# Splitting the last chunk's down projection by tokens: 384 with features on the partitions, 128 with tokens on the partitions

## The chip, the cores and the metric

The kernel runs on one core of one Trainium2 chip. The metric is the device time of one execution in microseconds (us); the kernel before has a median of 2044.64 us over 3 runs (2043.89 to 2045.69). Lower is better. TensorE does the matrix products and transposes into PSUM, VectorE (DVE) and ScalarE (ACT) the elementwise work, GpSimd (POOL) some products and the accumulating DMAs, and SyncE (SP) issues most DMAs, in the order in which they were written down.

## The reference

One layer of an encoder on 512 tokens with 2048 features in float32: a mixer (convolution and neighbourhood attention), then a gated MLP, then a final RMSNorm. The change touches only the last lines:

```python
up = depthwise_conv(jnp.einsum("bsd,df->bsf", xn, w_up[l]), ffn_dw_w[l], ffn_dw_b[l])
gate, val = jnp.split(up, 2, axis=-1)
x = x + jnp.einsum("bsf,fd->bsd", jax.nn.silu(gate) * val, w_down[l])    # 5632 -> 2048
return rms_norm(x, final_norm_g)     # x * rsqrt(mean(x*x over features) + eps) * g
```

## The kernel before

Activations lie transposed: features on the 128 partitions, the 512 tokens along the free dimension. 2048 features are 16 tiles `x2[0..15]` of 128 x 512 each. The hidden dimension 5632 is 44 tiles of 128, taken in 11 chunks of 4 (`NCH`, `CH`).

Matrix products keep float32 accuracy with three fast matmuls: weight and activation are each split into a rounded high part and a low rest, and `mm3` (L123) adds high x high, high x low and low x high into one PSUM bank (lines L126, L127, L128). So one product of a 128 x 128 weight tile with 4 hidden tiles (`hs[0..3]`, each a pair high and low) is 12 matmuls.

For chunks 0 to 9 the down projection (`down`, L830) makes one PSUM bank of 128 features x 512 tokens per feature tile d, copies it (L841) and has POOL add it by an accumulating DMA onto the residual in DRAM (`xd[d]`, L842). The last of these, for d = 8 to 15, run at the very end of the loop, between them the weights of the last chunk are loaded (`last_weights`, L865: 8 DMAs of 512 KB, split into `dh` and `dl` by ACT at L870 and DVE at L871). The residual comes back from DRAM as `x2[d]` (`reload`, L861).

The last chunk is not added through DRAM. `half` (L896) is called for tokens 0 to 255, then for tokens 256 to 511. For each d it makes 12 matmuls with a moving operand of 256 tokens into a bank of the pool `psm` (3 banks), DVE adds the bank onto `x2[d]` (L903), ACT squares it (L168), and DVE adds the square to `acc` (L169). `rsqrt_steps` (L171) then sums `acc` over the partitions by matmuls with ones (`st`, L183), takes 1/sqrt(mean + eps) with one Newton step on 128 x 2 values (L188 to L193), and spreads the result to all partitions by a matmul with a diagonal matrix (`dg` L200, `rb` L204). `finish` (L883) multiplies two feature tiles with the gain g3 and with `rb` (L892 on DVE, or for some pairs L889 on ACT and L890 on POOL) and stores 128 x 2 x 256 values to the output (L894, from SP's queue).

The statistics and the finishing of the first half are written between the feature tiles of the second half (`first_half`, L916). Those of the second half stand after its last matmul: nothing else is left then.

The order of instructions on each engine is made by a scheduler from priorities in writing order; each engine then runs its own list strictly in that order.

Of the kernel before, what the change touches and what calls it, by code (L numbers as in the profile page):

```python
# [28 lines left out]
EPS = 1e-6  # L29

KD = D // P
# [7 lines left out]
NB = GW // BLK  # L39
KC0 = [0, 8, 24, 32]  # L40
H = S // 2
CH = 4
NCH = NF // CH
NT = 79
# [19 lines left out]


@with_exitstack
def layer(ctx: ExitStack, tc: tile.TileContext, xT, xG, w_in, w_v, w_out, w_up, w_down, par, tab, out):
# [55 lines left out]
    def mm3(ps, w, wk, mh, ml, start, stop):  # L123
        hi, lo = w[:2]
        a = slice(wk * P, (wk + 1) * P)
        nc.tensor.matmul(ps, hi[:, a], mh, start=start, stop=False)  # L126
        nc.tensor.matmul(ps, hi[:, a], ml, start=False, stop=False)  # L127
        return nc.tensor.matmul(ps, lo[:, a], mh, start=False, stop=stop)  # L128
# [34 lines left out]
    def sum_sq(acc, src, first, to=slice(0, S)):  # L163
        if first:
            nc.scalar.activation(acc, src, AF.Square)
        else:
            q = t2("sq")[:, to]
            nc.scalar.activation(q, src, AF.Square)  # L168
            nc.vector.tensor_add(acc, acc, q)  # L169

    def rsqrt_steps(accs, n, name, to=slice(0, S), keep=True, by_token=None):  # L171

        if not isinstance(accs, tuple):
            accs = accs,
        m = (to.stop - to.start) // P
        banks = [psa.tile([P, S], F32, tag="po", name="st")]
        if len(accs) > 1:
            banks.append(psa.tile([P, 2, S], F32, tag="sc", name="st")[:, 0])
        v, r, y = (sm.tile([P, S // P], F32, tag="rs" + c, name="rs" + c)[:, :m] for c in "vry")
        for b, acc in enumerate(accs):  # L180
            ps = banks[b][:, :m]
            for i in range(m):
                nc.tensor.matmul(ps[:, i:i + 1], acc[:, to.start + i * P:to.start + (i + 1) * P], ones[:, 0:1],  # L183
                                 start=True, stop=True)
            if b:
                nc.vector.scalar_tensor_tensor(v, ps, 1.0 / n, v, op0=ALU.mult, op1=ALU.add)
            else:
                nc.vector.tensor_scalar(v, ps, 1.0 / n, EPS, op0=ALU.mult, op1=ALU.add)  # L188
        nc.scalar.activation(r, v, AF.Sqrt)
# [3 lines left out]
        nc.vector.scalar_tensor_tensor(y, y, 1.5, r, op0=ALU.add, op1=ALU.mult)  # L193

        if by_token is not None:
            by_token.append(y)
        if not keep:
            dg = t2("dg")
            for i in range(m):
                nc.vector.tensor_scalar(dg[:, i * P:(i + 1) * P], ident, y[:, i:i + 1], None, op0=ALU.mult)  # L200
            yield
            both = [psa.tile([P, S], F32, tag="tr", name="rb", bufs=2)[:, :m * P] for _ in range(2)]
            for ps in both:
                nc.tensor.matmul(ps, ones, dg[:, :m * P], start=True, stop=True)  # L204
            return both

        yh, yl = (sm.tile([P, S // P], dt, tag="rs" + c, name="rs" + c) for c, dt in (("h", F32R), ("l", F32)))
        nc.vector.tensor_copy(yh, y)
        nc.vector.tensor_sub(yl, y, yh.bitcast(F32))
        ds = []  # L210
        for part in (yh.bitcast(F32), yl):
            ds.append(t2("dg", F32R))
            nc.vector.tensor_mul(ds[-1].rearrange("p (i k) -> p i k", k=P), ident.unsqueeze(1).broadcast_to([P, m, P]),
                                 part.unsqueeze(2).broadcast_to([P, m, P]))
        yield
        ps = psa.tile([P, S], F32, tag="po", name="st")
# [6 lines left out]
    def rsqrt_value(g):  # L223
        while True:
            try:
                next(g)
            except StopIteration as e:
                return e.value

    xs, x1 = [], []
    acc1 = t2("acc1")
# [41 lines left out]
    for step in ORDER:  # L275
        if step == "v":
            half = next(v_)
# [3 lines left out]
        i = next(a_ if step == "a" else q_)  # L281
# [265 lines left out]
    p, n = -1, 0  # L547
# [20 lines left out]
    x2 = []  # L568
# [124 lines left out]
    def down_units(c, i, at):  # L693

        n = U // CH
        if not c:
# [161 lines left out]
    n = CH  # L858
    x2, ws = [], []

    def reload(d):  # L861
        x2.append(t2("x2"))
        nc.sync.dma_start(x2[d], xd[d])
# [15 lines left out]
        last_weights(len(ws))  # L879
    for d in range(KD // 2, KD):  # L880
        reload(d)

    def finish(ds, r, to, apart=False):  # L883

        o = t2("fin").rearrange("p (i t) -> p i t", i=2)[:, :len(ds)]
        for i, d in enumerate(ds):
            x, g = x2[d][:, to], pc("g3", d)
            if apart:
                nc.scalar.activation(x, x, AF.Copy, scale=g)  # L889
                nc.gpsimd.tensor_mul(o[:, i], x, r)  # L890
            else:
                nc.vector.scalar_tensor_tensor(o[:, i], x, g, r, op0=ALU.mult, op1=ALU.mult)  # L892
        i = ds[0] % 2
        nc.sync.dma_start(out[to.start // H, ds[0] // 2][:, i:i + len(ds)], o)  # L894

    def half(to, between):  # L896

        acc = t2("acc3")
        for d in range(KD):
            ps = psm.tile([P, S], F32, tag="mm", name="pd")[:, to]  # L900
            for k in range(n):
                mm3(ps, ws[d], k, hs[k][0][:, to], hs[k][1][:, to], k == 0, k == n - 1)
            nc.vector.tensor_add(x2[d][:, to], x2[d][:, to], ps)  # L903
            if d < KD - 1:
                sum_sq(acc[:, to], x2[d][:, to], d == 0, to=to)
            else:
                q = t2("sq")
                nc.scalar.activation(q[:, to], x2[d][:, to], AF.Square)
            between(d)
        return rsqrt_steps((acc, q), D, "rstd3", to=to, keep=False)  # L910

    h0, h1 = slice(0, H), slice(H, S)
    stats, todo = half(h0, lambda d: None), [(d, d + 1) for d in range(0, KD, 2)]
    r0 = []

    def first_half(d):  # L916

        if d == 0:
            next(stats)
        elif d == 2:  # L920
            try:
                next(stats)
            except StopIteration as e:
                r0.append(e.value[0])
        elif d > 2 and d % 5 != 4 and todo:
            finish(todo.pop(0), r0[0], h0)

    r, rp = rsqrt_value(half(h1, first_half))
    assert not todo

    rb = t2("rb")[:, h1]
    nc.scalar.activation(rb, rp, AF.Copy)
    for ds in [(0,), (1,)] + [(d, d + 1) for d in range(2, KD, 2)]:
        apart = ds[0] in (4, 10)
        finish(ds, rb if apart else r, h1, apart)


def _cols(a):
# [66 lines left out]
```

## Time and profile before

| | us |
|---|---|
| median of 3 runs | 2044.64 (2043.89 to 2045.69) |
| profiled execution, its time | 2047.1 |
| its span, first to last instruction | 2045.3 |
| PE busy in the span | 2025.5 |
| DVE busy | 1672.8 |
| ACT busy | 1035.4 |
| POOL busy | 156.2 |
| first matmul of `half` starts | 1981.96 |
| last DVE add of a PSUM bank onto x2 (L903) starts | 2030.14 |

The profile is of one execution. Its span is 1.8 us shorter than that execution's time, and that execution is 2.46 us above the median of the runs. Times inside the profile count from the span's start. A matmul's row shows when it starts and how long it lasts, and consecutive matmuls overlap: what a matmul costs a full TensorE is the distance from its start to the next one's.

### The profile page before, as it was taken

Reading aid. Unit: us, or ns where it says so; the run is one execution under the profiler, and the core shown is the slowest. Engines: PE = TensorE matmul, PEld = TensorE weight load, DVE = VectorE, ACT = ScalarE, POOL = GpSimd, SP = SyncE. Lnnn points to the kernel's source line nnn. Section 1 sums busy time; section 2 is a strip of 40 time slices with the busy share of each in tenths; the row PEclk is TensorE's granted clock in tenths of the full one; section 3 lists DMA queues with packets and bytes.
Section 4 is the critical chain, followed back from the end, with each engine's and each line's share of the span. In section 5 each row is a group of like instructions: output and inputs, shape, how many; then the busy total and the mean of one; then the engine's idle time right before and its main releaser. Section 6 shows DMA issues by size and latency. Waiting matters only on the chain.

```text
span 2045.3 us, 28399 instructions
## 1 busy us (share of the span) xinstructions
PE 2025.5 (99%) x10752; PEld 1731.9 (85%) x10752; DVE 1672.8 (82%) x2319; ACT 1035.4 (51%) x1662; POOL 156.2 (8%) x186
## 2 busy tenths in 40 slices
PE   9999999999999999999999999999999999999997
PEld 7888888878888898888888888888888888888887
DVE  7986888878577898888888788788888888889876
ACT  6323234347346555555555555555554555555552
POOL 0000000000001001111111111111111111110110
PEclk9999999999999999999999999999999999999998
DMA  7232333336347435566566565665555566555682
GB/s 254 82 104 91 114 95 103 108 119 216 104 121 178 113 114 144 118 151 145 124 144 144 135 133 145 138 134 142 131 146 143 124 146 146 130 134 127 149 212 83
DMA packets 97209, 275.38 MB, mean 135 GB/s; under 512 B 10928, under 2 KB 11696, under 8 KB 97072
## 3 DMA queue, kind: packets, MB, share of 16 engines
q1 hardware_dynamic: 71712, 227.40, 36.6%
q0 software_dynamic: 25216, 46.15, 15.6%
q8 instruction: 85, 1.39, 0.3%
q14 instruction: 52, 0.43, 0.1%
q10 hardware_dynamic: 144, 0.01, 0.0%
HBM read 218.99 MB, written 54.53 MB: 134 GB/s over the span
## 4 chain that ended last, share of the span: by engine, by line
PE 95%; DVE 2%; ACT 1%; DMA 1%; issue 1%; SPq 0%; DVEq 0%; ACTq 0%
PE pu L723 25%; PE pu L728 13%; PE pd L128 8%; PE pd L126 8%; PE pd L127 8%; PE pj L128 5%; PE pj L127 5%; PE pj L126 5%; PE po L126 3%; PE po L127 3%; PE po L128 3%; PE pv L330 1%; PE pv L332 1%; PE pv L331 1%; PE pu L126 1%; PE pu L128 1%
## 5 line engine op out<-in xcount | busy, mean ns | idle before, releaser
L115 ACT ACTIVATE whi<-raw 128x1024 fp32r<-128x1024 f32 x364 | 384.9, 1059 | 506.2 <-PE pj L127 148.0
L116 DVE TENSOR_TENSOR wlo<-raw,whi 128x1024 fp32r<-128x1024 f32 x364 | 443.9, 1221 | 215.6 <-ACT whi L115 205.9
L723 PE MATMUL pu<-xc,whi 128*128 128x512 f32 x2240 | 574.9, 392 | 0.2 <-ACT pl L735 0.2
L723 PEld LDWEIGHTS pu<-xc,whi 128*128 128x128 f32 x2240 | 409.2, 189 | 74.3 <-ACT pl L735 0.5
L728 PEld LDWEIGHTS pu<-xc,wlo 128*128 128x128 f32 x2240 | 305.6, 190 | 21.9
L728 PE MATMUL pu<-xc,wlo 128*128 128x256 f32 x2240 | 312.3, 282 | 0.0
L128 PE MATMUL pd<-hh,wlo 128*128 128x512 f32 x640 | 249.2, 391 | 0.0
L127 PE MATMUL pd<-hl,whi 128*128 128x512 f32 x640 | 249.2, 389 | 0.0
L126 PE MATMUL pd<-hh,whi 128*128 128x512 f32 x640 | 248.9, 391 | 0.0
L842 POOL DMA_DIRECT2D x2d<-pdc x160 | 139.2, 872 | 1169.6 <-ACT pdc L841 1051.5
L127 PE MATMUL pj<-xl,whi 128*128 128x512 f32 x512 | 200.4, 391 | 0.1
L128 PE MATMUL pj<-xh,wlo 128*128 128x512 f32 x512 | 200.0, 391 | 0.0
L126 PE MATMUL pj<-xh,whi 128*128 128x512 f32 x512 | 198.6, 392 | 0.4 <-ACT xh L267 0.4
L735 ACT ACTIVATE pl<-pu 128x256 f32<-128x256 f32 x280 | 104.4, 382 | 168.6 <-PE pu L723 168.5
L115 ACT ACTIVATE whi<-ws 128x1024 fp32r<-128x1024 f32 x132 | 139.6, 1058 | 76.9 <-PE pu L723 55.3
L384 DVE SCALAR_TENSOR_TENSOR y<-ch,prm,y 128x500 f32<-128x500 f32 (+14 forms) x240 | 173.4, 741 | 4.5
L116 DVE TENSOR_TENSOR wlo<-ws,whi 128x1024 fp32r<-128x1024 f32 x132 | 160.8, 1218 | 19.7 <-ACT whi L115 19.6
L128 PEld LDWEIGHTS pd<-hh,wlo 128*128 128x128 f32 x640 | 120.1, 188 | 28.8 <-DVE wlo L116 3.0
L127 PEld LDWEIGHTS pd<-hl,whi 128*128 128x128 f32 x640 | 120.3, 188 | 25.0
L126 PEld LDWEIGHTS pd<-hh,whi 128*128 128x128 f32 x640 | 120.5, 188 | 21.9
L841 ACT ACTIVATE pdc<-pd 128x512 f32<-128x512 f32 x160 | 93.8, 588 | 84.1 <-PE pd L128 84.1
L126 PEld LDWEIGHTS pj<-xh,whi 128*128 128x128 f32 x512 | 96.0, 188 | 22.3 <-issue 1.7
(188 smaller groups left out, 2911.3 us busy)
## 6 DMA issues: line engine op xcount, KB each, us to landing
raw<-in_w_up SPq DMA_DIRECT2D x176, 512.0 KB, 3.7
raw<-in_w_down SPq DMA_DIRECT2D x88, 512.0 KB, 4.0
x2d<-pdc POOLq DMA_DIRECT2D x160, 256.0 KB, 4.8
raw<-in_w_in SPq DMA_DIRECT2D x60, 512.0 KB, 3.7
raw<-in_w_out SPq DMA_DIRECT2D x32, 512.0 KB, 3.7
raw<-in_w_v SPq DMA_DIRECT2D x16, 512.0 KB, 4.0
tab<-in_tab SPq DMA_DIRECT2D x32, 256.0 KB, 5.1
x<-in_xG SPq DMA_DIRECT2D x16, 256.0 KB, 5.3
```

Source lines behind the costliest of these rows:

```text
L115: i = nc.scalar.activation(hi[:, :n], raw[:, :n], AF.Copy)
L116: j = nc.vector.tensor_sub(lo[:, :n], raw[:, :n], hi[:, :n].bitcast(F32))
L126: nc.tensor.matmul(ps, hi[:, a], mh, start=start, stop=False)
L127: nc.tensor.matmul(ps, hi[:, a], ml, start=False, stop=False)
L128: return nc.tensor.matmul(ps, lo[:, a], mh, start=False, stop=stop)
L330: nc.tensor.matmul(ps, xh, wh[:, f], start=kk == 0, stop=False)
L384: nc.vector.scalar_tensor_tensor(y[:, a:b], h[:, a + j - PAD:b + j - PAD], prm[:, o + j:o + j + 1], y[:, a:b], op0=ALU.mult, op1=ALU.add)
L723: return nc.tensor.matmul(ps, w[0][:, k * P:(k + 1) * P], comb[c][k], start=k == 0, stop=k == U - 1)
L728: nc.tensor.matmul(ps[:, H:], w[1][:, k * P:(k + 1) * P], comb[c][k][:, :H], start=False, stop=False)
L735: nc.scalar.activation(to, ps, AF.Copy)
L841: nc.scalar.activation(t, ps, AF.Copy)
L842: nc.gpsimd.dma_start(xd[d], t, accum_op=ALU.add)
```

## The change

The last chunk's tokens are divided otherwise: 384 (`LT`) and 128.

- For tokens 0 to 383 the same loop over d makes 12 matmuls with a moving operand of 384 tokens; add, square and sum follow as before, on 384 columns. Statistics of these tokens come from one call of `rsqrt_steps`, now with the diagonal matrices split in a high and a low part (2 matmuls into one bank, for all uses). One result in PSUM (`rb[0]`) is used by DVE, a copy of it in SBUF (`rb[1]`) by POOL. `finish` stores 128 x 2 x 384 values for each of 8 pairs.
- For tokens 384 to 511 the tokens go on the partitions. Four PSUM banks hold 128 tokens x 512 features each. Into each go first four transposes of `x2[d][:, 384:512]` (float32, by the matrix of ones on the diagonal), then 12 matmuls onto them, with the hidden tile as the stationary operand (128 tokens) and the weights as the moving one (512 features). The sum of squares of a token then lies along the free dimension: ACT squares a bank with a running sum (`accum_out`), DVE multiplies the bank by the gain, which comes from DRAM spread over the partitions (`g3b`, four loads of 256 KB), and when all four banks are in, one 128 x 1 column gives the factor; two banks are scaled by DVE, two by ACT, and stored.
- `spread` writes the statistics and the finishing of the 384 tokens between the matmuls of the four banks.
- The last chunk's weights are put in another order on the host, so that the weights of one hidden tile for four feature tiles lie side by side.

The order of the built program, against the one before, is the same up to the last chunk, but for one thing: the transposes for the first bank stand between the earlier down products of d = 12 and d = 13. On PE the four banks come in the order 0, 2, 1, 3; the `st` matmuls stand after 8 of bank 0's 12 matmuls, the two spreading matmuls after 9 and 11 of bank 2's, and bank 1's transposes wait for DVE's product on bank 0. On DVE the finishing of tiles 0, 1, 4, 5, 6, 7 and 10 stands between the products on banks 0 and 1.

```diff
-    def rsqrt_steps(accs, n, name, to=slice(0, S), keep=True, by_token=None):
+    def root(r, y, v):      # sqrt, reciprocal and the Newton step, as before
+    def rsqrt_steps(acc, n, name, to=slice(0, S), keep=True, by_token=None):
...
-        if not keep:
-            dg = t2("dg")
-            for i in range(m):
-                nc.vector.tensor_scalar(dg[:, i * P:(i + 1) * P], ident, y[:, i:i + 1], None, op0=ALU.mult)
-            yield
-            both = [psa.tile([P, S], F32, tag="tr", name="rb", bufs=2)[:, :m * P] for _ in range(2)]
-            for ps in both:
-                nc.tensor.matmul(ps, ones, dg[:, :m * P], start=True, stop=True)
-            return both
...
         for i, dg in enumerate(ds):
             nc.tensor.matmul(ps, ones_r, dg, start=i == 0, stop=i == 1)
+        if not keep:
+            return ps
...
+    gains = []
+    for g in range(CH):
+        gains.append(t2("g3b"))
+        nc.sync.dma_start(gains[g], g3[:, g * S:(g + 1) * S])
+    fm, tm = slice(0, LT), slice(LT, S)
...
+    acc = t2("acc3")
+    for d in range(KD):
+        ps = psm.tile([P, S], F32, tag="mm", name="pd")[:, fm]
+        for k in range(n):
+            mm3(ps, ws[d // CH * CH + k], d % CH, hs[k][0][:, fm], hs[k][1][:, fm], k == 0, k == n - 1)
+        nc.vector.tensor_add(x2[d][:, fm], x2[d][:, fm], ps)
+        sum_sq(acc[:, fm], x2[d][:, fm], d == 0, to=fm)
...
+    def spread(g, k):
+        if (g, k) == (0, 1):
+            next(stats)
+        elif (g, k) == (1, 1):
...
+            rb.append(t2("rb")[:, fm])
+            nc.scalar.activation(rb[1], rb[0], AF.Copy)
+        elif rb and pairs:
+            at = pairs.pop(0)
+            finish(at, rb[at % 3 == 1], at % 3 == 1)
+
+    for g, ps in enumerate(banks):
+        for i in range(CH):
+            nc.tensor.matmul(ps[:, i * P:(i + 1) * P], x2[g * CH + i][:, tm], ident, start=i == 0, stop=False,
+                             is_transpose=True)
+        for k in range(n):
+            (hh, hl), (dh, dl) = hs[k], ws[g * CH + k]
+            nc.tensor.matmul(ps, hh[:, tm], dh, start=False, stop=False)
+            nc.tensor.matmul(ps, hl[:, tm], dh, start=False, stop=False)
+            nc.tensor.matmul(ps, hh[:, tm], dl, start=False, stop=k == n - 1)
+            spread(g, k)
+        nc.scalar.activation(t2("sq"), ps, AF.Square, accum_out=sums[:, g:g + 1])
+        xg.append(t2("xg"))
+        nc.vector.tensor_mul(xg[g], ps, gains[g])
...
+    nc.vector.scalar_tensor_tensor(v, sums[:, CH - 1:], 1.0 / D, v, op0=ALU.mult, op1=ALU.add)
+    root(r, y, v)
+    for g in range(CH):
+        if g % 2:
+            nc.scalar.activation(xg[g], xg[g], AF.Copy, scale=y)
+        else:
+            nc.vector.tensor_scalar(xg[g], xg[g], y, None, op0=ALU.mult)
+        nc.sync.dma_start(last_out[:, g * S:(g + 1) * S], xg[g])
```

More of the change, by code (lines that the diff above doesn't have):

```diff
@@ L41 @@
 H = S // 2
+LT = S - P
 CH = 4
@@ L66, in layer @@
 @with_exitstack
-def layer(ctx: ExitStack, tc: tile.TileContext, xT, xG, w_in, w_v, w_out, w_up, w_down, par, tab, out):
+def layer(ctx: ExitStack, tc: tile.TileContext, xT, xG, w_in, w_v, w_out, w_up, w_down, par, tab, g3, out, last_out):
     nc = tc.nc
@@ L169, in sum_sq @@
             nc.vector.tensor_add(acc, acc, q)
-    def rsqrt_steps(accs, n, name, to=slice(0, S), keep=True, by_token=None):
[L173 to L181, printed above, removed]
-            for i in range(m):
[L183 to L188, printed above, removed]
+    def root(r, y, v):
         nc.scalar.activation(r, v, AF.Sqrt)
@@ L193, in rsqrt_steps @@
         nc.vector.scalar_tensor_tensor(y, y, 1.5, r, op0=ALU.add, op1=ALU.mult)
+    def rsqrt_steps(acc, n, name, to=slice(0, S), keep=True, by_token=None):
+        m = (to.stop - to.start) // P
+        ps = psa.tile([P, S], F32, tag="po", name="st")[:, :m]
+        v, r, y = (sm.tile([P, S // P], F32, tag="rs" + c, name="rs" + c)[:, :m] for c in "vry")
+        for i in range(m):
+            nc.tensor.matmul(ps[:, i:i + 1], acc[:, to.start + i * P:to.start + (i + 1) * P], ones[:, 0:1],
+                             start=True, stop=True)
+        nc.vector.tensor_scalar(v, ps, 1.0 / n, EPS, op0=ALU.mult, op1=ALU.add)
+        root(r, y, v)
         if by_token is not None:
             by_token.append(y)
-        if not keep:
-            dg = t2("dg")
-            for i in range(m):
-                nc.vector.tensor_scalar(dg[:, i * P:(i + 1) * P], ident, y[:, i:i + 1], None, op0=ALU.mult)
-            yield
-            both = [psa.tile([P, S], F32, tag="tr", name="rb", bufs=2)[:, :m * P] for _ in range(2)]
-            for ps in both:
-                nc.tensor.matmul(ps, ones, dg[:, :m * P], start=True, stop=True)
-            return both
-        yh, yl = (sm.tile([P, S // P], dt, tag="rs" + c, name="rs" + c) for c, dt in (("h", F32R), ("l", F32)))
+        yh, yl = (sm.tile([P, S // P], dt, tag="rs" + c, name="rs" + c)[:, :m] for c, dt in (("h", F32R), ("l", F32)))
         nc.vector.tensor_copy(yh, y)
@@ L215, in rsqrt_steps @@
         yield
-        ps = psa.tile([P, S], F32, tag="po", name="st")
+        ps = psa.tile([P, S], F32, tag="po", name="st")[:, :m * P]
         for i, dg in enumerate(ds):
             nc.tensor.matmul(ps, ones_r, dg, start=i == 0, stop=i == 1)
+        if not keep:
+            return ps
         res = t2(name)
@@ L881, in layer, with finish @@
         reload(d)
[L883 to L887, printed above, removed]
+    gains = []
[3 more added lines that the diff above has]
+    fm, tm = slice(0, LT), slice(LT, S)
+    def finish(pair, r, apart):
+        o = t4([P, 2, LT], "fin")
+        for i in range(2):
+            d = 2 * pair + i
+            x, g = x2[d][:, fm], pc("g3", d)
             if apart:
@@ L892, in finish @@
                 nc.vector.scalar_tensor_tensor(o[:, i], x, g, r, op0=ALU.mult, op1=ALU.mult)
[L893 to L918, printed above, removed]
+        nc.sync.dma_start(out[pair], o)
+    acc = t2("acc3")
[5 more added lines that the diff above has]
+        sum_sq(acc[:, fm], x2[d][:, fm], d == 0, to=fm)
+    wide = psa.tile([P, 2, S], F32, tag="sc", name="pt")
+    banks = [wide[:, 0], wide[:, 1]] + [psa.tile([P, S], F32, tag="tr", name="pt", bufs=2) for _ in range(2)]
+    stats, rb, xg = rsqrt_steps(acc, D, "rstd3", to=fm, keep=False), [], []
+    sums, v, r, y = (sm.tile([P, CH], F32, tag="rs" + c, name="rs" + c) for c in "lvry")
+    v, r, y = (t[:, :1] for t in (v, r, y))
+    pairs = list(range(KD // 2))
+    def spread(g, k):
+        if (g, k) == (0, 1):
             next(stats)
-        elif d == 2:
+        elif (g, k) == (1, 1):
             try:
@@ L923, in first_half @@
             except StopIteration as e:
[L924 to L935, printed above, removed]
+                rb.append(e.value)
+            rb.append(t2("rb")[:, fm])
[16 more added lines that the diff above has]
+        nc.vector.tensor_mul(xg[g], ps, gains[g])
+        if g == CH - 2:
+            nc.vector.tensor_reduce(v, sums[:, :CH - 1], axis=AX.X, op=ALU.add)
+            nc.vector.tensor_scalar(v, v, 1.0 / D, EPS, op0=ALU.mult, op1=ALU.add)
+    assert not pairs
+    nc.vector.scalar_tensor_tensor(v, sums[:, CH - 1:], 1.0 / D, v, op0=ALU.mult, op1=ALU.add)
+    root(r, y, v)
+    for g in range(CH):
[4 more added lines that the diff above has]
+        nc.sync.dma_start(last_out[:, g * S:(g + 1) * S], xg[g])
 def _cols(a):
```

21 lines of the change are left out of this document (10 added, 11 removed).

## The prediction

> **What bounds the kernel now.** The page first, for which engine carries the span; then the windows of the last stretch.
>
> ```profile
> PE 2025.5 (99%) x10752; PEld 1731.9 (85%) x10752; DVE 1672.8 (82%) x2319; ACT 1035.4 (51%) x1662; POOL 156.2 (8%) x186
> 2020.00:2030.00 10.00, 10.00 (x85) 9.90 (x83) 8.63 (x23) 3.94 (x9) 0.00 (x0) 1.00 0.39 146
> 2030.00:2040.00 10.00, 3.17 (x13) 2.14 (x12) 7.00 (x22) 1.00 (x3) 2.77 (x4) 0.63 0.24 87
> 2040.00:2046.00 6.00, 0.00 (x0) 0.00 (x0) 0.00 (x0) 0.00 (x0) 0.00 (x0) 0.50 0.61 228
> ```
>
> A window's row gives its length, busy time of PE, weight loads, DVE, ACT and POOL, the granted clock, the DMA share and GB/s. TensorE is full until 2030 at clock 1.00. After that it has nothing to multiply, and 15 us follow in which others finish. The change works in both: in the product from 1981.96 on (named PE time below) and in this tail. The chain of waits gives the tail (start, length, engine, tile, line):
>
> ```profile
> 2030.14 0.42 DVE x L903
> 2031.04 1.04 PE st L183 x8
> 2033.32 0.50 DVE dg L200 x2
> 2033.95 1.21 PE rb L204 x2
> 2035.18 0.48 DVE fin L892
> 2036.05 3.92 DVE fin L892 x10
> ```
>
> From the last add (2030.14) to the first finished tile (2035.18) are 5.04 us of statistics, then 4.79 us of finishing to 2039.97, then the stores until 2045.3: 15.2 us in all. What the changed kernel has after its last matmul is compared with these.
>
> **PE time of the products.** The timeline of PE, first column start, second length:
>
> ```profile
> 1979.69 0.39 PE L128 MATMUL pd<-hh,wlo 128*128 128x512 f32 x1
> 1981.73 0.39 PE L128 MATMUL pd<-hh,wlo 128*128 128x512 f32 x1
> 1981.96 0.28 PE L126 MATMUL pd<-hh,dh 128*128 128x256 f32 x1
> 1985.07 0.28 PE L128 MATMUL pd<-hh,dl 128*128 128x256 f32 x1
> 256.10 1.47 PE L499 MATMUL trp<-ident,tab 128*128 128x128 f32 x12
> 257.33 0.48 PE L126 MATMUL pj<-xh,whi 128*128 128x512 f32 x1
> 257.65 0.39 PE L127 MATMUL pj<-xl,whi 128*128 128x512 f32 x1
> 2006.43 0.50 PE L183 MATMUL st<-ones,acc 128*128 128x1 f32 x4
> 2007.24 0.36 PE L126 MATMUL pd<-hh,dh 128*128 128x256 f32 x1
> ```
>
> Nine matmuls of 512 columns lie between the first two: 2.04 / 9 = 0.2267 us each. 26 of 256 columns lie between the next two: 3.11 / 26 = 0.1196. A matmul of 384 columns is not in the trace; I take the middle, 0.1731, because the two ends differ almost by columns alone (0.107 for 256 columns). Its bounds are the two ends. Twelve transposes of 128 x 128 take 1.23 us, 0.103 each, and the first matmul after them costs 0.09 more than 0.227. Eight `st` matmuls take 0.81, 0.10 each.
>
> Removed: 2 x 192 matmuls of 256, 45.9 us. Added: 192 of 384, 33.2; 48 of 512 columns, 10.9; 16 transposes, 1.65; six `st` instead of sixteen, 0.6; two spreading matmuls of 384, 0.35; some 0.5 for five changes between the kinds. That is 47.2, against 45.9 plus 0.8 for the first half's `st` and about as much as the chain's `rb` row (1.21, at a lower clock) for its `rb`: 47.9. By bounds: at 0.1196 for 384 columns 10.3 less, at 0.2267 10.3 more. The product gets hardly shorter; the gain must come from the tail.
>
> [...]
>
> **Do its waits hold?** I walk the built order with the lengths of these groups (out<-in, shapes, count, busy us, mean ns); 384 columns are put halfway between 256 and 512.
>
> ```profile
> L903 DVE TENSOR_TENSOR x<-x,pd 128x256 f32<-128x256 f32 x32 | 13.3, 417 | 13.3 <-PE pd L128 13.0
> L169 DVE TENSOR_TENSOR acc<-acc,sq 128x512 f32<-128x512 f32 x29 | 19.9, 687 | 1.9 <-ACT ao L520 0.5 <-ACT sq L168 0.2
> L168 ACT ACTIVATE sq<-x 128x256 f32<-128x256 f32 x28 | 11.7, 418 | 26.6 <-DVE x L903 25.5 <-DVE rsy L193 1.1
> L168 ACT ACTIVATE sq<-x 128x512 f32<-128x512 f32 x15 | 8.2, 616 | 0.0
> L189 ACT ACT_TABLE_LOAD x5 | 6.4, 1283 | 0.1
> L213 DVE TENSOR_TENSOR dg<-ident,rsh 128x512 fp32r<-128x512 f32 x5 | 3.4, 684 | 0.0
> L433 DVE TENSOR_TENSOR q<-pj,rstd 128x512 f32<-128x512 f32 x8 | 5.5, 682 | 5.3 <-PE pj L128 5.3
> L892 DVE SCALAR_TENSOR_TENSOR fin<-x,prm,rb 128x256 f32<-128x256 f32 x28 | 12.4, 473 | 1.4 <-PE rb L204 1.4
> L268 DVE SCALAR_TENSOR_TENSOR xl<-x,g,xh 128x512 fp32r<-128x512 f32 x16 | 11.2, 749 | 5.5 <-ACT xh L267 5.4
> L890 POOL TENSOR_TENSOR fin<-x,rb 128x256 f32<-128x256 f32 x4 | 2.8, 718 | 50.7 <-ACT rb L932 50.7
> L380 DVE TENSOR_SCALAR y<-ch,prm 128x512 f32<-128x512 f32 x8 | 4.4, 545 | 0.2
> L159 ACT ACTIVATE mah<-y,prm 128x512 fp32r<-128x512 f32 x8 | 5.7, 711 | 0.0
> L487 ACT ACTIVATION_READ_ACCUMULATOR tab<-tab,nm 128x1 f32 x64 | 12.0, 187 | 0.0
> 1963.55 3.82 SPq L863 DMA_DIRECT2D x<-x2d  x8
> x<-x2d SPq DMA_DIRECT2D x4, 256.0 KB, 4.4
> ```
>
> First wait: the early transposes stand on PE at 1973.8 (after the down product of d = 12) and need `x2[0..3]`. The eight reloads are issued from 1963.55 in 3.82 us, so the fourth by about 1965.5, and the first four land 4.4 us after issue: 1970. Nothing waits; if it did, all of PE would stand behind it.
>
> So the 384s begin at 1981.96 + 0.41 + 0.09 = 1982.5 and end at 2015.7. Eight of bank 0's matmuls carry PE to 2017.5. The `st` behind them needs the last square sum: add 0.55 (417 to 687), square 0.52 (418 to 616), sum 0.55, with short hops, 2017.75. PE stands 0.2 us. After `st`, 2018.4. Four matmuls, bank 2's transposes and nine more bring PE to 2021.85, where it wants the first diagonal matrix. ACT has loaded its table (1.28) by 2018.9; root, Newton step and split on DVE give the two matrices (0.55 each) at 2020.9 and 2021.4. Spread by 2022.8. Bank 1's transposes want DVE's product on bank 0 (0.68, right after the matrices, 2022.1) and come up at 2023.2. The cover is about 1 us each time; were both gone by 1 us, the end would come up to 2 us later. Banks 1 and 3 take 5.8 us: last matmul ends 2029.5, against 2030.1 before. The gain loads (4 x 256 KB) follow the reloads on SP, when the queue has 20 us to spare.
>
> **The new tail, by the chain.** After 2029.5: ACT's square 0.62 and the reading of its sum 0.19; DVE's product 0.68, which stands ahead of the sum on DVE and may start 0.3 late behind the finishing of tile 13: 2031.35. The small steps from there to the factor are those of this timeline, first row to `dg` at 2033.32, 1.22 us:
>
> ```profile
> 2032.10 0.16 DVE L186 SCALAR_TENSOR_TENSOR rsv<-st,rsv 128x2 f32<-128x2 f32 x1 [0.29 <-PE st L183]
> 2035.69 6.01 SPq L894 DMA_DIRECT2D out_T<-fin  x9
> GB/s 0 0 0 0 0 127 320 246 257 4 0 0 0 97 395 380 365 387 380 395 380 358 402 373 402 372 358 402 387 387 372 82 0 0 0 0 0 0 0 0
> ```
>
> Factor at 2032.6. Two scalings each on DVE (0.55) and ACT (0.71) side by side: 2034.0; last store issued by 2034.4. Before, the last store issue ended at 2035.69 + 6.01 = 2041.7 and the span 3.6 us later. So the chain gives 2038.0. What went: the second statistics' spreading matmuls and, above all, finishing of half of the output after the last matmul; a quarter is left, in four pieces.
>
> **The new tail, by the stores.** The last row is the rate in 40 slices of 0.275 us from 2035 on: about 380 GB/s is the most the stores reach, first bytes 0.75 us after the first issue, last bytes some 1.6 us ahead of the end. All 4.19 MB of output now go out after one point: SP's first store is the pair that POOL makes. ACT's copy of the factors is ready at 2023.35, POOL's two products take 0.72 to 1.08 each (718 for 256 columns, half as much again for 384; I take 1.0): 2025.45. Then 0.75 + 4.19 / 0.38 = 11.0 us, 2037.2, and 1.6: 2038.8. Pairs come faster than they can be stored, so the queue doesn't run dry. That is 0.8 later than the chain; I take the later one.
>
> **Sum.** Span 2045.3 - 2038.8 = 6.5 us less; the profiled execution of 2047.1 would be 2040.6. The profiled one is 2.46 above the median; I take the difference off the median: 2044.64 - 6.5 = **2038.1 us**. One part in 500 (4.1 us) is about what a measurement can tell from no change: faster means below 2040.55, slower above 2048.73.
>
> **Rivals.**
>
> *The matmul of 384 columns is not halfway.* At the price of 512 (0.2267) the product grows by 10.3 us, everything behind it shifts: 2048.4. Slower than before from 0.207 on (6.5 / 192 = 34 ns more). For it: no row of 384. Against: 256 and 512 lie on one line through almost nothing. 0.06, mostly within the 0.2%.
>
> *The stores run slower* (the one that ends on the other side). All output now crosses one stretch; if it moves at the 228 GB/s of the last window's row instead of 380, 4.19 MB take 18.4 us instead of 11.0, and the end is 2045.5, slower than before; below 242 GB/s it decides against the change, below 194 GB/s by over 0.2%. For it: rows of 2 KB at a stride of 8 KB for the last part, none such in the trace. Against: 380 held for 5 us with the same queue. 0.06.
>
> *The clock falls.* The window from 2030 to 2040, in which PE mostly idles, shows 0.63 granted; 16 transposes and a stall now lie in the last stretch of products, and if they let the clock go like that for half of the banks' 13.8 us, 6.9 us become 10.9: 2042.1. All of it at 0.63 would give 2046.2. [...] Against it stands a window with 16 transposes at clock 1.00:
>
> ```profile
> 256.00:260.00 4.00, 4.00 (x27) 3.31 (x26) 1.82 (x2) 3.17 (x6) 0.00 (x0) 1.00 0.20 29
> ```
>
> Twelve of them stood in one block there, here never over seven. Chance 0.05.
>
> *DVE or ACT becomes the bound in the banks' stretch.* DVE has ten finishings (0.61 each, 0.53 apart), four products and the small steps between 2021 and 2032, about 9 of 11 us; if they run 3 us late, the last product does: 2040.5 to 2041.5. Chance 0.08.
>
> **Chances.** Forecast 0.75 (2035.5 to 2040.5). Faster 0.79: the forecast and half of the DVE case. Same 0.16: the other half, the clock, and most of the first two rivals. Slower 0.05: the far ends of those two. Range 2035.0 to 2042.0: below, 384 columns at 0.160 instead of 0.173 (2.5 us) and POOL's products at 0.72 each (0.6); above, the two covers lost (2) and POOL or the stores another 2 late, or the DVE or the clock case.
>
> **What would show it.** In the profile after: 384-column matmuls 0.173 apart; last matmul within 1 us of 2029.5; first output store near 2025.5 and about 380 GB/s from then until two us before the end; a span near 2038.8. Wrong, if PE shows idle time over 1 us before `st`, the spreading matmuls or bank 1's transposes, if the clock leaves 1.00 before 2029, or if the stores show holes.

## The result, and the profile after

The changed kernel has a median of 2038.87 us over 7 runs (2037.47 to 2039.84), the one before 2045.57 over 7 runs (2043.89 to 2046.74): a ratio of 0.9966, with a 95% interval of 0.9957 to 0.9976, or 6.70 us less. The forecast was 6.5 us less, 2038.1. The profiled execution of the changed kernel took 2039.84, with a span of 2038.1.

First the page's busy times of the changed kernel, then its windows (length; busy time of PE, weight loads, DVE, ACT, POOL; granted clock, DMA share, GB/s), cut where the 384-column products, the banks' products and the tail begin:

```profile
PE 2021.4 (99%) x10608; PEld 1727.4 (85%) x10608; DVE 1664.6 (82%) x2278; ACT 1036.9 (51%) x1658; POOL 159.7 (8%) x188
1982.00:2015.00 33.00, 33.00 (x192) 33.00 (x191) 18.09 (x33) 13.20 (x25) 0.88 (x1) 1.00 0.35 96
2015.00:2028.70 13.70, 13.65 (x69) 10.82 (x67) 9.67 (x24) 5.08 (x11) 5.42 (x6) 1.00 0.24 92
2028.70:2038.10 9.40, 0.00 (x0) 0.00 (x0) 3.07 (x11) 2.22 (x5) 0.51 (x1) 0.65 0.82 313
```

TensorE is full, at clock 1.00, until 2028.7. What follows it is 9.4 us long, where it was 15.2; and in it the engines do little (DVE 3.07), while the DMA share is 0.82. The tail is now mostly stores. PE's timeline (start, length):

```profile
1972.94 0.60 PE L910 MATMUL pt<-ident,x 128*128 128x128 f32 x4
1973.29 0.48 PE L127 MATMUL pd<-hh,whi 128*128 128x512 f32 x1
1981.57 0.33 PE L127 MATMUL pd<-hh,dh 128*128 128x384 f32 x1
2014.70 0.33 PE L129 MATMUL pd<-hh,dl 128*128 128x384 f32 x1
2014.87 0.39 PE L914 MATMUL pt<-dh,hh 128*128 128x512 f32 x1
2016.49 0.40 PE L915 MATMUL pt<-dh,hl 128*128 128x512 f32 x1
2016.92 0.80 PE L185 MATMUL st<-ones,acc 128*128 128x1 f32 x6
2021.11 0.34 PE L202 MATMUL st<-dg,ones 128*128 128x384 f32 x1
2021.75 0.34 PE L202 MATMUL st<-dg,ones 128*128 128x384 f32 x1
2022.16 0.93 PE L910 MATMUL pt<-ident,x 128*128 128x128 f32 x7
2028.30 0.39 PE L916 MATMUL pt<-dl,hh 128*128 128x512 f32 x1
```

None of these rows ends in a bracket, which is where the view notes a wait. 191 steps lie between the first and the last product of 384 columns: 33.13 / 191 = 0.1735 us each. The front of this execution came 0.9 us earlier than planned from the execution before (the first product of 384 columns at 1981.57, planned 1982.5); the front is the same program up to the four early transposes, so I measure everything from that row on. To the end of the span it is 56.5 us; before, from the first product of 256 columns at 1981.96, it was 63.3.

The rest of the tail, from the timelines of DVE, POOL, ACT and SP, and the rate of the DMAs in 40 slices of 0.525 us from 2020 on:

```profile
2019.93 0.55 DVE L197 TENSOR_TENSOR dg<-ident,rsl 128x384 fp32r<-128x384 f32 x1
2020.40 0.69 DVE L920 TENSOR_TENSOR xg<-pt,g3b 128x512 f32<-128x512 f32 x1
2022.65 3.76 DVE L876 SCALAR_TENSOR_TENSOR fin<-x,prm,st 128x384 f32<-128x384 f32 x7 [1.57 <-ACT rb L903]
2022.70 3.95 POOL L874 TENSOR_TENSOR fin<-x,rb 128x384 f32<-128x384 f32 x4 [39.06 <-ACT rb L903]
2024.72 6.27 SPq L877 DMA_DIRECT2D out_T<-fin  x8
2026.59 0.69 DVE L920 TENSOR_TENSOR xg<-pt,g3b 128x512 f32<-128x512 f32 x1 [0.18 <-ACT sq L918]
2029.22 0.19 ACT L918 ACTIVATION_READ_ACCUMULATOR sq<-pt 128x1 f32 x1
2029.49 0.68 DVE L920 TENSOR_TENSOR xg<-pt,g3b 128x512 f32<-128x512 f32 x1
2031.10 0.16 DVE L177 SCALAR_TENSOR_TENSOR rsy<-rsy,rsr 128x1 f32<-128x1 f32 x1
2031.81 2.54 SPq L932 DMA_DIRECT2D out_N<-xg  x4
GB/s 0 0 31 0 0 0 0 0 0 0 164 386 416 386 404 386 410 392 386 404 404 392 392 392 410 367 394 386 379 375 363 4 0 0 0 0 0 0 0 0
```

The stores start at 2024.72 with the pair that POOL makes, and from 2025.5 to 2036.3 there is no hole in the rate: some 390 GB/s. The four last stores, of the 128 turned tokens, are issued from 2031.81 on, into a queue that is still full.

### The profile page after: what moved, and what is told of

Read it like the earlier page. It is cut to its first block, busy times and chain, and to the rows that moved or that the text cites. A ratio compares the mean times of both kernels' runs of the same rounds, so it can differ in the third digit from the quotient of the medians.

```text
span 2038.1 us, 28060 instructions
## 1 busy us (share of the span) xinstructions
PE 2021.4 (99%) x10608; PEld 1727.4 (85%) x10608; DVE 1664.6 (82%) x2278; ACT 1036.9 (51%) x1658; POOL 159.7 (8%) x188
## 4 chain that ended last, share of the span: by engine, by line
PE 95%; DVE 2%; ACT 1%; issue 1%; DMA 0%; ACTq 0%; DVEq 0%
PE pu L700 25%; PE pu L705 13%; PE pd L129 8%; PE pd L127 8%; PE pd L128 8%; PE pj L127 5%; PE pj L129 5%; PE pj L128 5%; PE po L127 3%; PE po L129 3%; PE po L128 3%; PE pv L307 1%; PE pv L309 1%; PE pv L308 1%; PE pu L127 1%; PE pu L128 1%
## 5 line engine op out<-in xcount | busy, mean ns | idle before, releaser
L116 ACT ACTIVATE whi<-ws 128x1024 fp32r<-128x1024 f32 x132 | 139.7, 1059 | 76.8 <-PE pu L700 55.2
```

The source lines that it names most:

```text
L116: i = nc.scalar.activation(hi[:, :n], raw[:, :n], AF.Copy)
```

## The experiments

Two theories on the new end. **Stores**: all 4.19 MB cross one stretch that begins with SP's first store, and that sets the end (so the prediction had it). **Chain**: what follows the last matmul (square, gain, factor, scaling, four stores) sets it, and the stores are hidden. And two on where the gain comes from: the split at 384, or the turning of the rest. The effects are near 1 us, which is less than the timed ratios resolve (their intervals are 4 to 5 us wide); the verdicts rest on this table, in which each time counts from the first product of 384 columns in the same execution. Each row is one profiled execution; the span is known to a tenth, so the last three columns are good to 0.05.

| kernel | first store issued | last matmul ends | first of the four last stores issued | end | end less first store | end less four last stores |
|---|---|---|---|---|---|---|
| changed | 43.15 | 47.12 | 50.24 | 56.53 | 13.38 | 6.29 |
| changed, again | 43.12 | 47.10 | 50.21 | 56.49 | 13.37 | 6.28 |
| half the stores | 43.16 | 47.12 | 50.24 | 55.46 | 12.30 | 5.22 |
| earlier first store | 42.25 | 47.12 | 50.24 | 55.67 | 13.42 | 5.43 |
| shorter chain | 43.12 | 47.10 | 49.95 | 56.49 | 13.37 | 6.54 |
| no transposes | 43.14 | 45.77 | 49.96 | 56.53 | 13.39 | 6.57 |
| both small edits | 42.25 | 47.12 | 49.97 | 55.72 | 13.47 | 5.75 |
| two copies | 41.14 | 47.51 | 50.32 | 55.68 | 14.54 | 5.36 |
| split pair | 41.70 | 47.10 | 49.95 | 55.42 | 13.72 | 5.47 |

**The changed kernel again.**

> The changed kernel once more, unchanged, to see how far the time from the first product of 384 columns to the end of the span repeats: 56.5 within 0.1 if differences of 0.8 between the variants are to mean anything; if it comes out 0.5 or more away, the comparisons of 0.8 to 1.1 us are worth little.

56.49 against 56.53 (2039.32 us median, ratio 0.9968, 0.9956 to 0.9980). Every column repeats within 0.04 in these two executions, so differences of 0.3 mean something here.

**Half of the stores.**

```diff
-        nc.sync.dma_start(out[pair], o)
+        if pair not in (2, 3, 4, 6):
+            nc.sync.dma_start(out[pair], o)
```

> The changed kernel without the stores of four of the eight finished tile pairs (pairs 2, 3, 4 and 6, 1.57 of 4.19 MB; they are computed all the same). The time from the first product of 384 columns to the end of the span was 56.5 us in the changed kernel and 63.3 before. Theory 1, the stores set the end: with 2.62 MB left they are through before the chain is, so the end falls to what the chain behind the last matmul gives, some 1.8 us earlier: 54.7 (54.2 to 55.2), and the DMA rate runs dry before the last four stores. Theory 2, the chain behind the last matmul sets the end and the stores are hidden: 56.5 (within 0.3).

55.46 (2038.30 us, 0.9966, 0.9954 to 0.9978): the end moves 1.07 us, with the chain's issue times unchanged. The stores do set the end in the changed kernel; but what lies behind them is 1.07 away, not 1.8. SP's rows and the rate from 2020 on, in the same slices as above:

```profile
2032.18 1.80 SPq L933 DMA_DIRECT2D out_N<-xg  x4
GB/s 0 0 0 0 31 0 0 0 0 0 0 275 410 386 398 29 0 322 392 392 386 6 0 0 82 374 382 375 386 382 16 0 0 0 0 0 0 0 0 0
```

Now there are holes, and the last 1.05 MB run alone in the last block: 5.22 us from the first of these issues to the end. From the end of the last matmul that is 8.34 us.

**An earlier first store**: POOL takes other pairs, so that the first on the queue is one that DVE makes.

```diff
-            finish(at, rb[at % 3 == 1], at % 3 == 1)
+            finish(at, rb[at in (2, 4, 6)], at in (2, 4, 6))
```

> The changed kernel with GpSimd taking the pairs 2, 4 and 6 in place of 1, 4 and 7, so that the first pair on the store queue is not one that waits for GpSimd. Theory 1, the stores set the end and their start counts: the first store is issued some 0.9 us earlier, and the end comes 0.6 to 0.9 us earlier: 55.6 to 55.9 from the first product of 384 columns to the end, against 56.5. Theory 2, the chain behind the last matmul sets the end: 56.5 (within 0.3).

```profile
1980.43 0.33 PE L127 MATMUL pd<-hh,dh 128*128 128x384 f32 x1
2022.68 6.36 SPq L877 DMA_DIRECT2D out_T<-fin  x8
2030.67 1.85 SPq L932 DMA_DIRECT2D out_N<-xg  x4
```

The first store is issued 0.90 us earlier, the end comes 0.86 earlier (2038.23 us median, 0.9967, 0.9956 to 0.9979), and the last four stores are issued at the same 50.24. That is the stores theory to the tenth.

**A shorter chain.**

```diff
-        nc.vector.tensor_mul(xg[g], ps, gains[g])
+        if g < CH - 1:
+            nc.vector.tensor_mul(xg[g], ps, gains[g])
...
-    for g in range(CH):
-        if g % 2:
+    for g in (3, 1, 0, 2):
+        if g == 3:
+            nc.vector.scalar_tensor_tensor(xg[g], banks[g], y, gains[g], op0=ALU.mult, op1=ALU.mult)
+        elif g:
```

> The changed kernel with a shorter chain behind the last matmul: VectorE's product of the last bank with the gains (0.68 us ahead of the sum of squares) is taken out and joined to the scaling, which then reads the bank itself; the last stores go out in the order 3, 1, 0, 2. Theory 1, the stores set the end: the factor comes 0.6 us earlier and the end doesn't move, 56.5 (within 0.3) from the first product of 384 columns to the end. Theory 2, the chain sets the end: 55.9 (55.7 to 56.1).

```profile
1979.91 0.33 PE L127 MATMUL pd<-hh,dh 128*128 128x384 f32 x1
2023.03 6.28 SPq L877 DMA_DIRECT2D out_T<-fin  x8
2029.86 2.81 SPq L935 DMA_DIRECT2D out_N<-xg  x4
```

The four last stores are issued 0.29 us earlier, and the end stays (56.49; 2038.77 us, 0.9971, 0.9960 to 0.9982): they only stand in the queue for longer, 6.54 instead of 6.29. At the stores the edit gave half of the 0.6 that I had put: the factor does come 0.62 earlier, but the first scaling, which now reads the bank, takes DVE 0.75 instead of 0.44.

**No transposes.**

```diff
-        for i in range(CH):
-            nc.tensor.matmul(ps[:, i * P:(i + 1) * P], x2[g * CH + i][:, tm], ident, start=i == 0, stop=False,
-                             is_transpose=True)
...
-            nc.tensor.matmul(ps, hh[:, tm], dh, start=False, stop=False)
+            nc.tensor.matmul(ps, hh[:, tm], dh, start=k == 0, stop=False)
```

> The changed kernel without the 16 transposes that put the residual of the last 128 tokens under the product (for these tokens the residual is left out). TensorE's stretch gets 16 x 0.103 = 1.65 us shorter and up to 0.4 more for the changes between the kinds; the early four lie ahead of the first product of 384 columns, so 1.2 to 1.5 of that lie in the measure from there to the end. Theory 1, the stores set the end: their start hangs on the statistics of the first 384 tokens, not on these matmuls, except for bank 2's transposes ahead of the spreading matmuls (0.4 to 0.5 us): end at 56.0 (55.8 to 56.5). Theory 2, the chain behind the last matmul sets the end: 55.1 (54.9 to 55.4).

The last matmul ends 1.35 us earlier, and the end doesn't move (56.53; 2039.12 us, 0.9972, 0.9962 to 0.9983). The first store didn't move either, against my 0.5: in PE's list the spreading matmuls then stand behind more of the banks' products (the first behind 23, not 21), and come at the same time (39.53 us behind the first product of 384 columns, 39.54 in the changed kernel). And the four last stores came only 0.28 earlier, not 1.35. PE's last row, and two pieces of the chain of waits, show why:

```profile
2026.65 0.39 PE L913 MATMUL pt<-dl,hh 128*128 128x512 f32 x1
2028.47 0.52 DVE fin L876
2029.00 0.60 DVE xg L917
```

The last bank is full at 2027.04, and DVE comes to its gain product at 2029.00, behind finishings of the 384 tokens. In the changed kernel DVE's last wait in this stretch was the 0.18 us at 2026.59; from there on it was busy up to the last bank's product. So DVE was as good as the bound there already, and of TensorE's 1.35 us only 0.28 came through.

**The split alone** (before, cut at 384 and 128, all with features on the partitions).

```diff
+LT = S - P
...
-    h0, h1 = slice(0, H), slice(H, S)
+    h0, h1 = slice(0, LT), slice(LT, S)
```

> The kernel before with its halves cut at 384 and 128 tokens in place of 256 and 256, features on the partitions in both: the split alone, nothing turned. Theory 1, the gain needs the turned product, because with features on the partitions VectorE still adds, sums and finishes tile by tile: beside the 128-token products (192 of them, some 13 us) it has 16 additions, 15 sums and 16 finishings of 384 columns, 16 x 0.25 + 15 x 0.25 + 16 x 0.61 = 17.5 us, so TensorE is no longer the bound there, and the statistics of 5 us still follow: 63 to 67 us from the first product of 384 columns to the end, no gain against the 63.3 of the kernel before. Theory 2, the gain comes from the smaller rest alone (a quarter of the output left after the last matmul): 2.4 us less of finishing and some 2 less of stores, 58.5 to 60.

2057.87 us (2054.51 to 2062.46), ratio 1.0061 (1.0042 to 1.0080): slower than before by 13 us, and in the profile 78.8 us from the first product to the end. Worse than either theory said. The four executions differ more than those of other kernels: two took 2054.5 and 2054.9 at a mean granted clock of 0.996, two 2060.9 (the profiled one) and 2062.5 at 0.993 and 0.992. Even the shortest is 9.5 us slower than before. PE's timeline and the windows:

```profile
2016.33 0.27 PE L128 MATMUL pd<-hl,dh 128*128 128x128 f32 x1
2018.78 0.28 PE L129 MATMUL pd<-hh,dl 128*128 128x128 f32 x1
2028.52 0.33 PE L127 MATMUL pd<-hh,dh 128*128 128x128 f32 x1 [0.94 <-DVE x L904]
2028.00:2030.00 2.00, 1.48 (x13) 1.48 (x13) 1.92 (x6) 0.77 (x3) 0.00 (x0) 0.96 0.94 366
2030.00:2032.00 2.00, 2.00 (x11) 2.00 (x10) 0.98 (x4) 0.88 (x3) 0.00 (x0) 0.50 0.59 228
```

22 steps lie between the first two rows: 0.111 us for a product of 128 columns, hardly less than the 0.1196 of 256. So the line through 256, 384 and 512 columns doesn't go on below 256. 192 of them cost 21.4 us where I had taken some 13. What sets this floor no run shows. On top of that the granted clock falls to 0.50 near 2030 and stays there to the end of the products (0.50 in both windows of 10 us from 2030 to 2050; the last product ends at 2048.17).

**The split alone, without finishing.**

```diff
-            finish(todo.pop(0), r0[0], h0)
+            todo.pop(0)
```

> The kernel with the split alone, whose time from the first product of 384 columns to the end was 78.8 us, 15.5 more than before the change, with the granted clock at 0.50 from 2030 on; here the finishing and the stores of the 384 tokens are left out. Theory 1: VectorE's finishing made TensorE wait for a free bank (1.2 us in two waits), and the waits brought the clock down. Without them the clock stays at 1.00 to the last product, the 192 products of 128 columns take 0.111 each as in the clock-1.00 part, and the end is at 33.2 + 21.4 + 2.6 + some 10.5 = 67.7 (66.5 to 69). Theory 2: products of 128 columns bring the clock down by themselves, since TensorE's array is used less in them: the clock falls to 0.50 some 15 us into them all the same, and the end is at 74 to 79.

71.3 us (2053.32 us median, 1.0037, 1.0023 to 1.0051), between the two, and neither theory is right as put. The windows around the fall and the return of the clock, and one near the end of the products:

```profile
2015.00:2016.00 1.00, 1.00 (x11) 1.00 (x11) 0.16 (x1) 1.00 (x1) 0.00 (x0) 1.00 0.00 0
2016.00:2016.50 0.50, 0.50 (x6) 0.50 (x6) 0.17 (x1) 0.27 (x2) 0.00 (x0) 1.00 0.00 0
2016.50:2017.00 0.50, 0.50 (x6) 0.50 (x5) 0.44 (x3) 0.00 (x0) 0.00 (x0) 0.68 0.11 33
2017.00:2018.00 1.00, 1.00 (x6) 1.00 (x6) 0.96 (x6) 0.31 (x1) 0.00 (x0) 0.50 0.00 0
2023.00:2023.50 0.50, 0.50 (x4) 0.50 (x4) 0.00 (x0) 0.00 (x0) 0.00 (x0) 0.50 0.00 0
2023.50:2024.00 0.50, 0.50 (x6) 0.50 (x6) 0.00 (x0) 0.00 (x0) 0.00 (x0) 1.00 0.00 0
2038.00:2040.00 2.00, 2.00 (x21) 2.00 (x19) 0.87 (x3) 0.43 (x2) 0.00 (x0) 1.00 0.00 0
```

The clock fell here too, although TensorE waited for nothing (busy for the whole of each window), for 6.8 us; then it stayed at 1.00 through 16 us of products of 128 columns. So the waits are not needed for a fall, and the narrow products alone don't make one. Ahead of this fall lie twelve `st` matmuls of one column, ahead of the other 0.94 us of waiting. The sums alone don't make a fall either: with the split alone the same twelve stand at 2014.88, and the clock stays at 1.00 until 2029.8. The 67.7 of the first theory and the 3.4 us that 6.8 at half the clock lose are 71.1, near the 71.3 measured. What decides is open, and these readings of the clock rest on one profiled execution of each kernel.

**The turning alone** (the changed kernel cut at 256, the rest as two groups of 128 tokens).

```diff
-LT = S - P
+LT = S // 2
...
+    for j in range((S - LT) // P):
+        tm = slice(LT + j * P, LT + (j + 1) * P)
```

> The changed kernel cut at 256 and 256 tokens: the first 256 with features on the partitions, then two groups of 128 turned. TensorE: 192 x 0.1196 + 96 x 0.2267 = 44.7 us for the matmuls, as 44.1 in the changed kernel, and 16 transposes more (1.65), some 2.0 us more in all up to the last matmul. Stores begin some 5 us earlier. Theory 1, in the changed kernel the stores set the end, 1.8 us behind the chain: here they start early enough, the chain sets the end, and the time is the chain's plus 2.0: 56.7 (56 to 57.5) from the first product of 256 columns to the end, against 56.5. Theory 2, the chain sets the end in both: 58.5 (58 to 59.2).

```profile
1982.48 0.28 PE L127 MATMUL pd<-hh,dh 128*128 128x256 f32 x1
2031.94 0.39 PE L919 MATMUL pt<-dl,hh 128*128 128x512 f32 x1
2033.09 0.69 DVE L923 TENSOR_TENSOR xg<-pt,g3b 128x512 f32<-128x512 f32 x1 [2.25 <-ACT sq L921]
```

2040.35 us, ratio 0.9977 (0.9968 to 0.9987): 58.1 us to the end, a tenth inside the range of the second theory. But that theory gave the right number for a wrong reason. The last matmul ends 49.85 behind the first, 2.7 us later than in the changed kernel, where I had put 2.0 (four more blocks of transposes bring changes between the kinds, which I left out; no run measures them apart). From its end to the span's end are 8.27 us, which is the 8.34 of the kernel with half the stores: in both the chain binds, here behind a queue that had been empty for some 8 us. DVE has no finishing left here, and its product on the last bank waits for ACT's square of it all the same (last row). With the sizes measured, the first theory's sum gives 55.46 + 2.73 = 58.2. Turning brings 5.2 of the 6.8 us (4.7 of 6.7 by the medians), and the larger first part the rest.

**Both small edits, and two more.** The first joins the earlier store and the shorter chain.

> Both small edits together: GpSimd takes the pairs 2, 4 and 6, and the last bank's product with the gains is joined to the scaling. Theory 1 (the stores set the end by some 1.8 us): only the earlier first store counts, 55.6 to 55.9 from the first product of 384 columns to the end, as with that edit alone. Theory 2 (the chain sets the end): 55.9, as with the shorter chain alone. If each is right in part, 55.2 to 55.6 and the fastest version so far.

55.72 (2038.72 us, 0.9965, 0.9952 to 0.9977): as with the earlier store alone, which is the first theory. To start the stores earlier still, the factors were spread into two banks and the first pair stored as two tiles:

```diff
-            nc.scalar.activation(rb[1], rb[0], AF.Copy)
+            nc.scalar.activation(rb[1], both[1], AF.Copy)
...
+            if not pair:
+                nc.sync.dma_start(out[pair][:, i], o[:, i])
+        if pair:
+            nc.sync.dma_start(out[pair], o)
```

> The changed kernel with the two small edits (GpSimd takes the pairs 2, 4 and 6; the last bank's gain product joined to the scaling), and two more that start the stores earlier: the factors of the 384 tokens are spread into two PSUM banks, so that VectorE's finishing doesn't stand behind ScalarE's copy of the bank (0.5 us), at the price of two more matmuls of 384 columns (0.35 us of TensorE), and the first pair is stored as two tiles (0.5 us). The stores would begin 1.0 us earlier than with the two small edits alone, whose end is bound by them at 55.7 us behind the first product of 384 columns. Theory 1 (stores, then the chain): the end moves until the chain binds. The chain behind the last matmul took 8.35 us where it bound, less 0.6 for the shorter chain, and the last matmul ends 47.1 + 0.35 behind the first: 55.2 (55.0 to 55.4). Theory 2 (something else holds the end at 55.5 to 55.7, such as the last stores' own way): no gain.

```profile
2020.86 1.21 SPq L881 DMA_DIRECT2D out_T<-fin  x2
2022.99 5.27 SPq L883 DMA_DIRECT2D out_T<-fin  x7
GB/s 31 0 0 263 141 339 6 281 415 375 404 386 427 380 392 392 421 392 386 404 277 378 390 382 379 371 8 0 0 0 0 0 0 0 0 0 0 0 0 0
2020.22 4.29 DVE L879 SCALAR_TENSOR_TENSOR fin<-x,prm,st 128x384 f32<-128x384 f32 x8 [1.17 <-PE st L205]
2026.84 0.39 PE L923 MATMUL pt<-dl,hh 128*128 128x512 f32 x1
```

DVE no longer waits for ACT's copy, the first store is 1.1 us earlier (41.14), and the end doesn't move: 55.68 (2037.57 us, 0.9963, 0.9950 to 0.9977). The rate (same slices) shows that the earlier start was not used: the queue ran dry between the first pair's two tiles and behind them (141 and 6 GB/s, 2022.1 to 2023.7), so first store to end took 14.54 instead of 13.4. It ran dry for a moment once more ahead of the four last stores (277 near 2030.8). The two more matmuls cost TensorE 0.39, so the last matmul and the four last stores come as much later, and from these to the end it takes 5.36: the chain binds now, by little, and at more than the 55.2 that I had put for it; most of that is the shorter chain, worth 0.3 and not 0.6. So I kept the split store and left the second copy out:

> The two small edits and the first pair stored as two tiles, without the second copy of the factors. So far, from the first product of 384 columns: the first store was issued at 42.25 with the two small edits, and from the first store to the end it took 13.4 us wherever the stores set the end (13.37 to 13.47 in five kernels); the first of the last four stores was issued at 49.97 and from there to the end it took 5.2 us where nothing was queued ahead of it (5.22 with half of the stores left out). Theory 1, the end is the later of these two: the first store moves to 41.7 (one finishing, 0.53, earlier), 41.7 + 13.4 = 55.1 against 49.97 + 5.22 = 55.2: end at 55.2 to 55.4, some 0.4 earlier than with the two small edits. Theory 2, the last four stores can't follow closer than 5.4 to 5.7 us while all the other stores stand ahead of them: 55.4 to 55.7, no gain.

```profile
2022.78 0.87 SPq L878 DMA_DIRECT2D out_T<-fin  x2
2024.20 5.28 SPq L880 DMA_DIRECT2D out_T<-fin  x7
GB/s 0 31 0 0 0 0 20 366 354 179 392 404 404 386 398 398 404 380 404 410 386 398 388 382 375 375 390 382 16 0 0 0 0 0 0 0 0 0 0 0
2031.03 1.83 SPq L938 DMA_DIRECT2D out_N<-xg  x4
```

55.42, where the two ranges meet: the first store is 0.55 earlier, the end 0.30. It is 1.1 us less than the changed kernel in the profile; the timed ratio, 0.9967 (0.9955 to 0.9979; median 2038.26), can't tell it from the changed kernel's. The rate shows where the rest went: one hole behind the split pair (179 GB/s near 2025), some 0.3 us, and none after it. So the stores still set the end, over 13.72 us. The four last ones took 5.47 behind a queue with a short backlog, 5.22 behind an empty one.

## Why the prediction was right

By its own steps, with 0.9 taken off its times for the earlier front.

- *384 columns halfway, 0.1731.* Measured 0.1735. With the 512s of bank 0 at (2016.49 - 2014.87) / 7 = 0.231, slightly over the 0.2267 that I took, the last matmul ends at 2028.69, forecast 2028.6. No run shows the 0.160 that the lower end of the range took for these matmuls; 0.1735 is what the runs showed.
- *Transposes, 0.103 each, and the changes between kinds.* Without the twelve that lie in the measure the last matmul ends 1.35 earlier; 12 x 0.103 is 1.24.
- *The early transposes wait for nothing.* They stand in PE's rows at 1972.94 with no wait, and the next product follows 0.35 later.
- *0.2 us in front of `st`.* From 2016.49 to 2016.92 are 0.43, a step of 0.23 and 0.2 of standing.
- *The diagonal matrices, with 1 us of cover.* The second is done at 2020.48; PE takes the first at 2021.11 and the second at 2021.75. Bank 1's transposes start at 2022.16 behind a product on DVE that ended at 2021.09. Both covers were there.
- *POOL's pair as first store, 2024.55.* POOL took 0.99 for each of its four products (3.95 / 4; I took 1.0), and the first store was issued at 2024.72.
- *The stores' stretch: 0.75 + 11.0 + 1.6 = 13.35.* It was 13.37 to 13.39 in the four kernels with this first store, 13.42 and 13.47 in two with an earlier one. The rate was some 10 GB/s higher than the 380 that I took; the pieces at both ends made that up.
- *The stores 0.8 later than the chain.* 1.07 by the kernel with half the stores. The chain's own length, 8.5 from the last matmul, was 8.34, but two of its terms were off and cancelled, which is luck: the factor came 2.6 behind the last matmul (forecast 3.1), since rows that I had added up overlap, and DVE started the last bank's product 0.08 behind ACT's reading of it (2029.41 to 2029.49) and not 0.3; and in the kernel with half the stores the issue of the last four ended 1.0 behind the last scaling, where I had 0.4. That the stores, and not the chain, set the end is what five experiments turned on, and it held.
- *The product hardly shorter, the gain from the tail.* First product to last 47.1 and 0.35 to 0.5 more for the early transposes, against some 48.1 before; the tail 9.4 against 15.2.

The difference of the medians, 6.70, and that of the sum, 6.5, agree; most of the 0.8 us by which the median missed is in the base, since the kernel before came out at 2045.57 in these runs, 0.93 above the median from which I took the difference off.

The rivals: the price of 384 columns was as taken; the stores did not slow down, and the rows of 2 KB at a stride of 8 KB moved at 374 to 386 GB/s; the clock stayed at 1.00 to the last matmul, with 16 transposes and the stall in the stretch. DVE did come level with TensorE, without the 2 us of slack that I had seen in its 9 busy of 11 us: it was busy from 2026.59 to the last bank's product, and the kernel without transposes shows it as the bound. It held that product up by 0.08 us, and the end by nothing, since the stores set it. The limit that I gave for slower stores is 239 GB/s by my own sum (4.19 MB in 11.0 + 6.5 us), not 242; it decides nothing. A step that I had not seen: DVE stands for 1.57 us ahead of its first finishing. The first 1.0 of that is for the spreading matmuls (the second ends at 2022.09), the other 0.5 for ACT's copy of the same bank, and with a second bank those 0.5 went. It cost nothing, because POOL's pair was the first store anyway.

## What to carry to other kernels

When work moves off the path behind the last matmul, add up the bytes that must leave after one point, and compare their stretch (issue, bytes by rate, landing) with the new chain: here they were 1 us apart, and only an edit at the later one moved the end. Turning the operands, so that the tokens are stationary and 512 features stream, is what makes a narrow remainder cheap: at clock 1.00 these 128 tokens take 48 products of 0.231, 11.1 us, and 16 transposes, some 1.7, against 192 of 0.111, 21.4 us, with features on the partitions, and that kernel was 9 to 17 us slower than the one before. Before you count a saving on TensorE as time, look which engine comes next: 1.35 us off the products brought 0.28 at the last stores.

## What the runs showed that I had not expected

- A product of 128 columns takes 0.111 us, 256 columns 0.1196, 384 0.1735: half the columns, from 256 to 128, save 7% in these kernels.
- The granted clock can fall to 0.50 while TensorE never waits: it did for 6.8 us in a stretch of 128-column products with one-column sums among them. In the run with waits it fell near 2029.9 and did not come back in 18 us of such products; at 0.50 one of them takes 0.213. Two of that kernel's four executions had a higher mean clock and were 6 to 8 us shorter.
- In the six kernels in which the stores set the end and the queue did not run dry, first store to end took 13.4 us for 4.19 MB, with a spread of 0.1, whatever was done elsewhere. An earlier first store brings less where the second comes late: 13.72 with one hole, 14.54 with two.
